# Gated delta rule in a fused decoder: gates as a process, weights split two units ahead, longer planned times for transfers, the turn bank's hold counted

## The chip, the cores and the metric
One core of a Trainium2 chip runs the whole program; the other cores are idle. The metric is the device time of one launch in microseconds, smaller is better. The core has a matrix engine (PE, with a weight-load stage PEld), VectorE (DVE), ScalarE (ACT), GpSimd (POOL), and SyncE (SP), whose queue issues most transfers. Engines run side by side, each takes its own instructions strictly in order, and they wait for each other by semaphores.

## The reference
Three decoder blocks, one after the other, on 512 tokens of width 1024, float32. The change lies in the second layer of the first block, `parallel_mixers`: a gated delta rule with 8 heads of 128 (tokens in chunks), beside a gated convolution of 31 taps over 1024 channels. Cut to that part:

```
proj = h @ w_in                      # qkv | z | a | bt | glu | gates
qkv = silu(causal_depthwise_conv(qkv, gdn_conv_qkv))          # 4 taps
g = -exp(gdn_a_log) * softplus(a + gdn_dt_bias); beta = sigmoid(bt)   # the decay gates: 16 columns of proj
gc = cumsum(g within a chunk); decay = exp(gc_i - gc_j) for i >= j
m = strict_lower((k*beta) k^T * decay)
u, w = solve(I + m, v*beta), solve(I + m, k*beta*exp(gc))
per chunk: v_new = u - w S;  o = (q*exp(gc)) S + (q k^T * decay) v_new
           S = S*exp(gc_last) + (k*exp(gc_last - gc))^T v_new
o = rms_norm(o) * silu(z)
c = c_lin * sigmoid(c_gate)          # the GLU: two halves of proj for each channel
c = silu(layer_norm(causal_depthwise_conv(c, conv_dw_w) + conv_dw_b))
y = sigmoid(g_a) * (o @ w_gdn_out) + sigmoid(g_c) * (c @ w_conv_out + b_conv_out)
```

## The kernel before
Every large product is made of three matmuls on split operands (`mm3`, lines L212 to L214: x by wl, x by wh twice): a weight tile of 1024 x 128 is loaded raw (`wr`, two buffers, SP's queue, `wload`, L353), cast to its high part `wh` on ACT (`split`, L346), and its low part `wl` is made by a subtraction (L347), in this stage on POOL, elsewhere on DVE. `wh` and `wl` have four buffers each.

The stage "gdn" is written as *units* and *processes*. A unit is one product of 1024 x 128 weights with all 512 tokens: 24 matmuls into one PSUM bank. There are 53 units after the start: q, k, v of heads 1 to 7 (`gdn_rows`), 16 GLU halves (`glu_conv`), 8 of z (`gdn_z`), 8 of output gates (`gdn_gate`). A process is a generator for the small, latency-bound work: it emits some instructions and yields a time in ns after which it may go on. `step` runs the process that is due, else three matmuls of the current unit. The clock of this planner is `pe_ns`, a sum of assumed PE times (680 ns for a triple, 230 for a small matmul, 110 for a turn); order of emission is order of execution on every engine except SP's queue (`keep_order`). So a yield is a number of PE nanoseconds, in the planner's count, that other work fills.

What the words stand for:
- *gates* (`gdn_gates`): the 16 columns a, bt become `small` (tile gsmall): beta, the cumulated decays (by matmuls with `triu` and `ones`) and their exponentials; they also go to DRAM as `gcrow`, from where each head's decay rows are fetched.
- *post* in `gdn_rows`: the 4-tap convolution (L824, L826), silu (L830, L833), a *turn* (four transposes, `four_turned`, L218) into the single PSUM bank of tag tp, from which ACT then copies (L837, L847) or sums squares (L814).
- *pairs*: for two heads at a time `gdn_decay`, then `gdn_blocks` (16 x 16 blocks inverted on DVE after a trip through DRAM: sm, sy, sx), `gdn_join` (blocks joined to 128 x 128), `gdn_head` (the recurrence and the final z product, L1052).
- *taps*: the 31-tap convolution is 30 DVE instructions per channel block (L654) and 8 blocks; `fill_dve` emits them one at a time wherever the planner thinks DVE is behind PE. Those left when all units are done are emitted behind the loop.
- *mix2*: the stage behind it starts with the products of the last gates (`gate_proj`, its low parts on DVE), then transposes the convolution's rows (`conv_norm`, L693), which need every tap done.

`split_ahead(2)` makes `wload` for the next units when one begins; a unit whose `may` is false is passed over for others, and one that comes up without its weights gets them on the spot:

```
        for u in ([u for u in units if u["may"]()] + units)[:n]:
            if u["w"] is None and sum(e["w"] is not None for e in units) < 3:
                u["w"] = wload(*u["src"])
```

Of the kernel before, what the change touches and what calls it, by code (L numbers as in the profile page):

```python
# [25 lines left out]
JOIN_NS, CHUNK_NS = 1300.0, 1300.0  # L26
# [82 lines left out]
def kernel(ctx: ExitStack, tc: tile.TileContext, a: dict, out: bass.AP, upto=99):  # L109
    nc = tc.nc  # L110
    V, A, G, PE, S = nc.vector, nc.scalar, nc.gpsimd, nc.tensor, nc.sync
    pe_ns, dve_ns = [0.0], [0.0]
# [181 lines left out]
    def unit(src, body, may=lambda: True):  # L294
        units.append({"src": src, "body": body, "may": may, "w": None})
# [341 lines left out]
    def glu_conv(c):  # L637
# [43 lines left out]
        unit((w, 0, 8, 4112 + 1024 + c * 128, 128), body, lambda: bool(ps))  # L681
# [40 lines left out]
    def gdn_gates():  # L722
# [3 lines left out]
        h, l = wload(w, 0, 8, 4096, 16)  # L726
        p = bank()
        for k in range(8):
            mm3(p[:16], (h[:, k], l[:, k]), (act.hi(k), act.lo(k)), k == 0, k == 7)
        ab = work("xr", (128, T))  # L730
        A.copy(ab[:16], p[:16])
        pt = tbank()
        for tt in range(4):
            PE.transpose(pt[:, tt, :16], ab[:16, tt * 128:(tt + 1) * 128], ident[:16, :16])
# [9 lines left out]
        V.tensor_tensor(u, u, z, OP.min)  # L744
        A.activation(u, u, AF.Exp)
        V.tensor_scalar(s2, u, 2.0, None, OP.add)
# [10 lines left out]
        ea = tiny((128, 8))  # L757
        A.activation(ea, alog, AF.Exp)
        V.scalar_tensor_tensor(sm(4), sm(4), -1.0, ea[:, None, :].to_broadcast([128, 4, 8]), OP.mult, OP.mult)
        pc = tbank((128, T))  # L760
        mm(pc[:, 0:32], triu, acc)
        mm(pc[:, 32:64], ones, acc)
        V.tensor_copy(small[:, 5], pc[:, 0:32])
        pr = tbank((128, T))
        PE.transpose(pr[:32, :128], small[:, 5], ident)
        row = t1()
        V.tensor_copy(row[:32], pr[:32, :128])
        gd["rows"] = dpool.tile([32, 128], FT, name="gcrow")
        S.dma_start(gd["rows"], row[:32])
# [7 lines left out]
        yield  # L777
# [9 lines left out]
    def gdn_rows(h):  # L787
# [18 lines left out]
        def four_turned(x):  # L806
            p = tbank()
            for c in range(4):
                turn(p[:, c], x[:, c], ident)
            return p  # L810
# [5 lines left out]
        def post(i, p):  # L816
# [18 lines left out]
            q = four_turned(xf)  # L835
# [9 lines left out]
            else:  # L845
# [7 lines left out]
                yield 3500.0  # L853
                A.copy(kq[:, :, 0], four_turned(s_))
# [27 lines left out]
    def gdn_decay(h):  # L882
        dt_ = t2((128, 4, 128))
        src = gd["rows"][0:1, 0:1]
        A.dma_start(dt_, bass.AP(tensor=src.tensor, offset=src.offset + h * 128, ap=[[0, 128], [1024, 4], [1, 128]]))
        yield 4000.0
# [22 lines left out]
    def gdn_blocks(h):  # L909
# [10 lines left out]
        yield 4000.0  # L920
# [20 lines left out]
        yield 4000.0  # L941
# [1032 lines left out]
    with ExitStack() as outer:  # L1974
        outer.enter_context(room(dict(ma=12)))
        mark("gdn")
        with room(vk=6, mt=4, at=4, Y=4, X=2, pad=2, xr=3, sq=1, t2=4, sqc=1, gsmall=1, ub=1, yb=1, tb=1):
            sq, lev = work("xr", (128, 3, 128)), work("sqc", (128, 2, 128))
# [12 lines left out]
            run(gdn_start(), gdn_gates())  # L1991
            banks(pj=3, tp=1, gt=3, cv=1)
            gdn_rows(0)
# [151 lines left out]
```

## Time and profile before

| | us |
|---|---|
| three runs: lowest, median, highest | 2883.54, 2889.5, 2892.16 |
| the profiled execution, its own time | 2888.98 |
| its span, first to last instruction | 2887.2 |
| PE busy over the span | 2704.2 (94%) |
| stage gdn and the first products of mix2, up to the last tap | about 402 to 1008 of the span |
| mean granted clock of TensorE | 0.966 |

The span is cut into stages by `mark`, and only the stretch from 402 to 1008 us differs between the two programs. The rows below have times in us from the span's start. In a timeline the bracket says how long the engine was idle just before the row and what ended that. [...]

### The profile page before, as it was taken

What the parts mean: (1) busy time and instruction counts of PE and PEld (TensorE: products, weight loads), DVE (VectorE), ACT (ScalarE), POOL (GpSimd) and SP (SyncE); (2) the same over time, 40 slices, a digit from 0 to 9 for tenths busy, and PEclk for the clock granted to TensorE, in tenths of its full rate; (3) what the DMA queues carried; (4) which work ended last, traced back from release to release, by engine and by line L of the source; (5) the groups of instructions that cost most, each with busy time, mean ns of one, the idle gap of its engine ahead of it and who ended that gap; (6) DMA issues with size and microseconds to landing.
All of it is one profiled execution on the core that took longest, in us unless ns stands there. A gap on an engine that the chain in (4) does not pass through costs nothing. (4 is left out here: it accounts for less than half of the span.)

```text
span 2887.2 us, 34809 instructions
## 1 busy us (share of the span) xinstructions
PE 2704.2 (94%) x13600; PEld 2193.2 (76%) x13600; DVE 1368.0 (47%) x2460; ACT 1066.4 (37%) x1999; POOL 477.7 (17%) x357
## 2 busy tenths in 40 slices
PE   9999978888889599999999999999999999999998
PEld 8888856667677488888888877776687777788887
DVE  3232354555546855655323256476454564622324
ACT  4222225444434242352322235455145564332231
POOL 0101025333333001101110121022001100311010
PEclk9999989889899799999999999999999999999999
DMA  5223334436454433444323323322235222443322
GB/s 187 95 99 98 95 90 78 76 63 72 62 89 43 75 99 126 125 147 146 110 95 96 102 94 113 111 59 82 71 100 99 56 70 74 130 141 97 101 95 80
DMA packets 330420, 277.30 MB, mean 96 GB/s; under 512 B 50360, under 2 KB 282512, under 8 KB 330256
## 3 DMA queue, kind: packets, MB, share of 16 engines
q1 hardware_dynamic: 292816, 251.22, 33.5%
q10 hardware_dynamic: 37440, 23.86, 2.7%
q8 instruction: 107, 1.75, 0.2%
q14 instruction: 57, 0.47, 0.1%
HBM read 256.64 MB, written 20.49 MB: 96 GB/s over the span
## 5 line engine op out<-in xcount | busy, mean ns | idle before, releaser
L212 PE MATMUL mm<-x,wl 128*128 128x512 f32 (+3 forms) x2072 | 813.5, 393 | 41.2 <-POOL wl L347 37.1
L347 DVE TENSOR_TENSOR wl<-wr,wh 128x1024 fp32r<-128x1024 f32 (+1 forms) x351 | 428.4, 1221 | 794.3 <-ACT wh L346 793.1
L213 PE MATMUL mm<-x,wh 128*128 128x512 f32 (+3 forms) x2072 | 798.7, 385 | 0.0
L214 PE MATMUL mm<-x,wh 128*128 128x512 f32 (+3 forms) x2072 | 797.7, 385 | 0.0
L346 ACT CAST wh<-wr 128x1024 fp32r<-128x1024 f32 (+2 forms) x425 | 436.3, 1027 | 804.4 <-PE mm L214 488.6
L212 PEld LDWEIGHTS mm<-x,wl 128*128 128x128 f32 (+2 forms) x2072 | 398.8, 192 | 120.4 <-POOL wl L347 40.6
L214 PEld LDWEIGHTS mm<-x,wh 128*128 128x128 f32 (+2 forms) x2072 | 398.5, 192 | 77.2 <-issue 1.9
L213 PEld LDWEIGHTS mm<-x,wh 128*128 128x128 f32 (+2 forms) x2072 | 399.8, 193 | 70.3 <-issue 1.4
L347 POOL TENSOR_TENSOR wl<-wr,wh 128x1024 fp32r<-128x1024 f32 x74 | 176.7, 2392 | 577.1 <-ACT wh L346 562.8
L347 POOL TENSOR_TENSOR h<-t,h 128x512 fp32r<-128x512 f32 x66 | 101.7, 1541 | 838.6 <-ACT h L346 838.6
L214 PE MATMUL mm<-wh,h 128*128 128x512 f32 x528 | 205.6, 389 | 0.0
L212 PE MATMUL mm<-wh,h 128*128 128x512 f32 x528 | 205.5, 389 | 0.0
L213 PE MATMUL mm<-wl,h 128*128 128x512 f32 x528 | 205.5, 389 | 0.0
L654 DVE SCALAR_TENSOR_TENSOR mm<-pad,cols,mm 128x512 f32<-128x512 f32 x232 | 174.7, 753 | 22.6 <-ACT mm L650 17.0
L214 PEld LDWEIGHTS mm<-wh,h 128*128 128x128 f32 x528 | 99.1, 188 | 20.6
L212 PEld LDWEIGHTS mm<-wh,h 128*128 128x128 f32 x528 | 99.1, 188 | 20.5
L213 PEld LDWEIGHTS mm<-wl,h 128*128 128x128 f32 x528 | 99.1, 188 | 20.5
L566 ACT ACTIVATE t<-mm 128x512 f32<-128x512 f32 x66 | 39.5, 599 | 127.9 <-PE mm L214 127.9
L826 DVE SCALAR_TENSOR_TENSOR xr<-mm,cols,xr 128x511 f32<-128x511 f32 (+2 forms) x72 | 53.8, 748 | 65.6 <-ACT xr L824 64.0
L567 DVE SCALAR_TENSOR_TENSOR t<-t,mm 128x512 f32<-128x512 f32 x66 | 45.4, 688 | 78.2 <-POOL h L347 54.9
L212 PE MATMUL mm<-m,wl 128*128 128x512 f32 (+1 forms) x224 | 81.6, 364 | 0.2 <-DVE g L1116 0.2
L214 PE MATMUL mm<-m,wh 128*128 128x512 f32 (+1 forms) x224 | 81.3, 363 | 0.0
(455 smaller groups left out, 3736.5 us busy)
## 6 DMA issues: line engine op xcount, KB each, us to landing
wr<-in_w_in SPq DMA_DIRECT2D x122, 512.0 KB
wr<-in_ffn_wg SPq DMA_DIRECT2D x44, 512.0 KB
wr<-in_ffn_wu SPq DMA_DIRECT2D x44, 512.0 KB
wr<-in_ffn_wd SPq DMA_DIRECT2D x44, 512.0 KB
wr<-in_w_ffn_in SPq DMA_DIRECT2D x44, 512.0 KB
wr<-in_w_ffn_out SPq DMA_DIRECT2D x22, 512.0 KB
xd<-m ACTq DMA_DIRECT2D x32, 256.0 KB
wr<-in_w_xkv SPq DMA_DIRECT2D x16, 512.0 KB
```

Of the source, the lines that this page charges most:

```text
L212: PE.matmul(o, lh[1], rh[0], start=start, stop=False)
L213: PE.matmul(o, lh[0], rh[1], start=False, stop=False)
L214: PE.matmul(o, lh[0], rh[0], start=False, stop=stop)
L346: A.copy(hi, src)
L347: (eng or V).tensor_sub(lo, src, hi.bitcast(FT))
L566: A.activation(sg, ps[0][f], AF.Silu)
L567: V.scalar_tensor_tensor(sg, sg, scale, ps[1][f], OP.mult, OP.mult)
L654: V.scalar_tensor_tensor(p if j < 30 else o, pad[:, j:j + T], tap31(j, c), p, OP.mult, OP.add)
L826: V.scalar_tensor_tensor(x[:, d:], p[:, :T - d], tap(3 - d), x[:, d:], OP.mult, OP.add)
```

## The change
The gates' product becomes a unit and their arithmetic a process (`gdn_decays`), which yields between its steps, so that units are emitted between them; its row of decays is issued from ACT's queue instead of SP's. Everything that reads the gates waits by a flag in the planner. The second half of a GLU pair may start (and have its weights split) at any time, and `split_ahead(2)` is called once before the loop. Yields get longer: joins and chunks 1300 to 1700, the decay rows 4000 to 6000, the blocks 4000 to 5000, Y and X 4000 to 7000, the turn of k 3500 to 5000. `tp_free` keeps the planner's time at which the turn bank will be read out; a turn waits for it. Two constants move from a buffer of xr to one of t2.

```diff
-JOIN_NS, CHUNK_NS = 1300.0, 1300.0
+JOIN_NS, CHUNK_NS = 1700.0, 1700.0
...
         unit((w, 0, 8, 4112 + c * 128, 128), body)
-        unit((w, 0, 8, 4112 + 1024 + c * 128, 128), body, lambda: bool(ps))
+        unit((w, 0, 8, 4112 + 1024 + c * 128, 128), body)
...
         dtb, alog = bcast_row("gdn_dt_bias", 8), bcast_row("gdn_a_log", 8)
-        h, l = wload(w, 0, 8, 4096, 16)
-        p = bank()
-        for k in range(8):
-            mm3(p[:16], (h[:, k], l[:, k]), (act.hi(k), act.lo(k)), k == 0, k == 7)
-        ab = work("xr", (128, T))
+
+        def body(h, l):
+            p = bank()
+            for k in range(8):
+                mm3(p[:16], (h[:, k], l[:, k]), (act.hi(k), act.lo(k)), k == 0, k == 7)
+                yield 1
+            spawn(post(p))
+
+        unit((w, 0, 8, 4096, 16), body)
...
+    def gdn_decays(p, dtb, alog):
+        ab = t2()
         A.copy(ab[:16], p[:16])
+        ea = tiny((128, 8))
+        A.activation(ea, alog, AF.Exp)
+        yield 1500.0
         pt = tbank()
+        tp_free[0] = pe_ns[0] + 4000.0
         for tt in range(4):
-            PE.transpose(pt[:, tt, :16], ab[:16, tt * 128:(tt + 1) * 128], ident[:16, :16])
+            turn(pt[:, tt, :16], ab[:16, tt * 128:(tt + 1) * 128], ident[:16, :16])
...
+        yield 1500.0
         A.activation(u, u, AF.Exp)
+        yield 2500.0
...
+        yield 6000.0
         pc = tbank((128, T))
+        tp_free[0] = pe_ns[0] + 3000.0
         mm(pc[:, 0:32], triu, acc)
         mm(pc[:, 32:64], ones, acc)
         V.tensor_copy(small[:, 5], pc[:, 0:32])
-        pr = tbank((128, T))
-        PE.transpose(pr[:32, :128], small[:, 5], ident)
-        row = t1()
-        V.tensor_copy(row[:32], pr[:32, :128])
-        gd["rows"] = dpool.tile([32, 128], FT, name="gcrow")
-        S.dma_start(gd["rows"], row[:32])
...
-        yield
+        yield 3000.0
+        pr = tbank((128, T))
+        turn(pr[:32, :128], small[:, 5], ident)
+        row = t1()
+        A.copy(row[:32], pr[:32, :128])
+        yield 1000.0
+        gd["rows"] = dpool.tile([32, 128], FT, name="gcrow")
+        A.dma_start(gd["rows"], row[:32])
+        yield 3000.0
+        gd["gates"] = True
...
-        def four_turned(x):
+        def four_turned(x, held):
             p = tbank()
+            tp_free[0] = pe_ns[0] + 440.0 + held
...
-            q = four_turned(xf)
+            yield from until(lambda: tp_free[0] <= pe_ns[0] and "beta" in gd)
+            q = four_turned(xf, 2500.0 if i == 0 else 1500.0)
...
-                yield 3500.0
-                A.copy(kq[:, :, 0], four_turned(s_))
+                yield 5000.0
+                yield from until(lambda: tp_free[0] <= pe_ns[0] and "kd" in gd)
+                A.copy(kq[:, :, 0], four_turned(s_, 1500.0))
...
     def gdn_decay(h):
+        yield from until(lambda: "gates" in gd)
...
-        yield 4000.0
+        yield 6000.0
...
         G.memset(yb.rearrange("p a b -> p (a b)")[:, ::17], 1.0)
-        yield 4000.0
+        yield 5000.0
...
                 gd["decay", h + i].append(m)
-        yield 4000.0
+        yield 7000.0
...
-            sq, lev = work("xr", (128, 3, 128)), work("sqc", (128, 2, 128))
+            sq, lev = t2((128, 3, 128)), work("sqc", (128, 2, 128))
...
-            run(gdn_start(), gdn_gates())
+            run(gdn_start())
             banks(pj=3, tp=1, gt=3, cv=1)
             gdn_rows(0)
+            gdn_gates()
             spawn(gdn_pair(0))
...
+            split_ahead(2)
             while True:
```

Where instructions stand, at three places. First PE at the stage's start, before: the last matmul of the gates' own product (mm_2795), their turn, the sums with triu and ones (L208), the turn to rows (L765), and then the first unit, the GLU half mm_2911.

```order
L214 MATMUL mm_2795<-x_2456,wh_2790 16x512
L734 MATMUL mm_2822<-ident,xr_2820 128x16 x4
L208 MATMUL mm_2858<-gsmall_2827,xr_2606 128x32 x2
L765 MATMUL mm_2862<-ident,gsmall_2827 32x128
L212 MATMUL mm_2911<-x_2444,wl_2895 128x512
L213 MATMUL mm_2911<-x_2445,wh_2894 128x512
```

Now the turn (of t_2852) stands inside the first GLU half, here mm_2862, and the sums stand 48 matmuls of units later, inside the unit mm_2962:

```order
L214 MATMUL mm_2862<-x_2444,wh_2796 128x512
L218 MATMUL mm_2872<-ident,t_2852 128x16 x4
L212 MATMUL mm_2862<-x_2444,wl_2797 128x512
L213 MATMUL mm_2862<-x_2445,wh_2796 128x512
L214 MATMUL mm_2862<-x_2444,wh_2796 128x512
```

```order
L214 MATMUL mm_2962<-x_2444,wh_2857 128x512
L208 MATMUL mm_2973<-gsmall_2877,t_2606 128x32 x2
L212 MATMUL mm_2962<-x_2444,wl_2858 128x512
L213 MATMUL mm_2962<-x_2445,wh_2857 128x512
L214 MATMUL mm_2962<-x_2444,wh_2857 128x512
```

So no two steps of the gates stand next to each other on PE any more; 12 matmuls lie between the sums and the next turn.

Second POOL at the same place, before: the low parts of the weights in the order in which they are made. wl_2895 is that of the first GLU half, wl_2945 that of its second half; L887 adds the mask to the decay rows of heads 0 and 1, which come from DRAM.

```order
L347 TENSOR_TENSOR wl_2895<-wr_2893,wh_2894 128x1024
L347 TENSOR_TENSOR wl_2901<-wr_2899,wh_2900 128x1024
L347 TENSOR_TENSOR wl_2907<-wr_2905,wh_2906 128x1024
L887 TENSOR_TENSOR t_2891<-t_2891,sqc_2607 128x512
L887 TENSOR_TENSOR t_2918<-t_2918,sqc_2607 128x512
L347 TENSOR_TENSOR wl_2945<-wr_2943,wh_2944 128x1024
```

Now the two halves' are wl_2797 and wl_2820:

```order
L347 TENSOR_TENSOR wl_2797<-wr_2795,wh_2796 128x1024
L347 TENSOR_TENSOR wl_2820<-wr_2818,wh_2819 128x1024
L347 TENSOR_TENSOR wl_2858<-wr_2856,wh_2857 128x1024
L347 TENSOR_TENSOR wl_2900<-wr_2898,wh_2899 128x1024
L347 TENSOR_TENSOR wl_2958<-wr_2956,wh_2957 128x1024
L667 TENSOR_TENSOR ma_2952<-ma_2952,xr_2954 128x512
```

The second half's low part moved from behind two weights and two mask additions to right behind the first's. The same holds for the other GLU pairs; one weight in the stage (the z product of head 4) is still made where its unit starts.

Third DVE at the stage's end, before: the last two heads' z products (L1052) and the taps and low parts (L347, of the first products of mix2) behind them.

```order
L1052 SCALAR_TENSOR_TENSOR ma_6545<-mm_6618,cols_286,ma_6545 128x512
L654 SCALAR_TENSOR_TENSOR mm_6416<-pad_6413,cols_300,mm_6416 128x512
L1052 SCALAR_TENSOR_TENSOR ma_6545<-mm_6631,cols_286,ma_6545 128x512
L654 SCALAR_TENSOR_TENSOR mm_6416<-pad_6413,cols_300,mm_6416 128x512 x13
L347 TENSOR_TENSOR wl_6864<-wr_6862,wh_6863 128x1024
L654 SCALAR_TENSOR_TENSOR mm_6416<-pad_6413,cols_300,mm_6416 128x512
```

Now (L1075 is the z product there):

```order
L1075 SCALAR_TENSOR_TENSOR ma_6564<-mm_6652,cols_286,ma_6564 128x512
L1075 SCALAR_TENSOR_TENSOR ma_6564<-mm_6658,cols_286,ma_6564 128x512
L654 SCALAR_TENSOR_TENSOR ma_4940<-pad_6337,cols_300,mm_6340 128x512
L654 SCALAR_TENSOR_TENSOR mm_6687<-pad_6684,cols_293,mm_6687 128x512 x10
L347 TENSOR_TENSOR wl_6864<-wr_6862,wh_6863 128x1024
L654 SCALAR_TENSOR_TENSOR mm_6687<-pad_6684,cols_293,mm_6687 128x512 x4
```

Behind the second z product 75 taps stood, and 61 stand now; eight low parts lie among them in both. On PE only six matmuls of a unit are left between the last head's last product (L208, with at) and its final turn, where 30 stood.

## Rows read from the trace of the kernel before

**Rows 1.** The page: busy time of the engines over the span, share, instructions.
```profile
PE 2704.2 (94%) x13600; PEld 2193.2 (76%) x13600; DVE 1368.0 (47%) x2460; ACT 1066.4 (37%) x1999; POOL 477.7 (17%) x357
```

**Rows 2.** Stretches of the stage: start:end, length, busy time (and instructions) of each engine, granted clock, share of the DMA engines, GB/s.
```profile
402.00:426.00 24.00, 7.42 (x33) 3.65 (x32) 11.80 (x40) 7.73 (x13) 2.70 (x2) 0.69 0.05 12
426.00:922.00 496.00, 419.42 (x2233) 341.20 (x2233) 260.29 (x531) 224.29 (x545) 185.58 (x127) 0.88 0.49 71
...
950.50:978.00 27.50, 27.45 (x121) 22.64 (x122) 24.94 (x32) 6.89 (x8) 0.00 (x0) 1.00 0.76 106
978.00:1008.50 30.50, 1.32 (x9) 0.79 (x8) 27.40 (x37) 6.39 (x12) 0.00 (x0) 0.55 0.09 26
```

**Rows 3.** What PE waited for from 427 to 922: us in total, times, longest.
```profile
PE mm L212 <- POOL wl L347: 29.1, 8, 5.7
PE mm L208 <- DMA X<-sx: 10.1, 2, 5.1
PE mm L218 <- ACT t L814: 9.0, 6, 2.4
PE mm L218 <- ACT Y L992: 6.2, 2, 3.6
PE mm L208 <- ACT t L1017: 5.2, 2, 4.2
...
PE mm L218 <- POOL sq L852: 4.4, 2, 4.0
```

**Rows 4.** PE in order of time around the gates.
```profile
406.89 0.39 PE L214 MATMUL mm<-x,wh 128*16 128x512 f32 x1
407.94 0.41 PE L734 MATMUL mm<-ident,xr 16*128 16x16 f32 x4 [0.67 <-ACT xr L731]
418.18 1.03 PE L208 MATMUL mm<-gsmall,xr 128*128 128x32 f32 x4 [9.82 <-issue]
...
425.70 0.79 PE L212 MATMUL mm<-x,wl 128*128 128x512 f32 x1 [5.81 <-POOL wl L347]
```

**Rows 5.** PE inside one unit, at the clock's lower level (start to start) and, four microseconds later, at the higher.
```profile
428.00 0.63 PE L214 MATMUL mm<-x,wh 128*128 128x512 f32 x1
428.43 0.63 PE L212 MATMUL mm<-x,wl 128*128 128x512 f32 x1
...
432.64 0.39 PE L212 MATMUL mm<-x,wl 128*128 128x512 f32 x1
432.87 0.39 PE L213 MATMUL mm<-x,wh 128*128 128x512 f32 x1
```

**Rows 6.** Three stretches in which the granted clock was at its lower level throughout (columns as in rows 2).
```profile
411.00:431.50 20.50, 7.23 (x19) 5.57 (x20) 9.34 (x35) 4.50 (x9) 4.66 (x2) 0.50 0.29 53
...
622.80:643.00 20.20, 15.89 (x64) 11.55 (x65) 6.68 (x9) 5.99 (x14) 2.35 (x1) 0.50 0.17 26
759.50:772.80 13.30, 12.86 (x57) 9.37 (x58) 8.95 (x12) 8.70 (x18) 2.37 (x1) 0.50 0.07 10
```

**Rows 7.** One weight from its issue on SP's queue to its cast and its low part; then the unit of the second GLU half, and the z product of head 4, which wait for theirs.
```profile
425.67 0.37 SPq L353 DMA_DIRECT2D wr<-in_w_in  x1
431.09 1.05 ACT L346 CAST wh<-wr 128x1024 fp32r<-128x1024 f32 x1 [6.91 <-DMA wr<-in_w_in]
432.21 2.40 POOL L347 TENSOR_TENSOR wl<-wr,wh 128x1024 fp32r<-128x1024 f32 x1 [4.24 <-ACT wh L346]
439.76 0.79 PE L212 MATMUL mm<-x,wl 128*128 128x512 f32 x1 [5.60 <-POOL wl L347]
831.69 0.80 PE L212 MATMUL mm<-x,wl 128*128 128x512 f32 x1 [5.74 <-POOL wl L347]
```

**Rows 8.** A cast that waits for its transfer, the PE instruction behind it, and the stretch around them (columns as in rows 2).
```profile
684.78 1.04 ACT L346 CAST wh<-wr 128x1024 fp32r<-128x1024 f32 x1 [7.83 <-DMA wr<-in_w_in]
686.15 0.58 PE L208 MATMUL mm<-t,vk 128*128 128x128 f32 x1 [4.15 <-ACT t L1017]
660.00:700.00 40.00, 30.29 (x139) 25.24 (x138) 18.79 (x36) 11.92 (x28) 16.21 (x11) 0.89 0.91 84
```

**Rows 9.** The fetch of X for heads 0 and 1 (issue) and its first reader; a step of a join on 32 x 32 blocks.
```profile
523.04 2.36 ACTq L939 DMA_DIRECT2D X<-sx  x2
531.14 1.22 PE L208 MATMUL mm<-X,mt 128*128 128x128 f32 x4 [4.98 <-DMA X<-sx]
876.00 1.48 PE L208 MATMUL mm<-Y,X 32*32 32x32 f32 x32 [2.82 <-ACT X L982]
```

**Rows 10.** PE at the end of head 6: the last product and the final turn.
```profile
913.00 0.38 PE L208 MATMUL mm<-t,at 128*128 128x128 f32 x2
920.07 0.60 PE L218 MATMUL mm<-ident,t 128*128 128x128 f32 x4
```

**Rows 11.** DVE behind the last z product, and the last channel block.
```profile
922.60 0.75 DVE L1052 SCALAR_TENSOR_TENSOR ma<-mm,cols,ma 128x512 f32<-128x512 f32 x1 [0.49 <-PE mm L218]
...
944.22 1.23 DVE L347 TENSOR_TENSOR wl<-wr,wh 128x1024 fp32r<-128x1024 f32 x1 [10.70 <-ACT wh L346]
...
984.66 22.92 DVE L654 SCALAR_TENSOR_TENSOR mm<-pad,cols,mm 128x512 f32<-128x512 f32 x29 [0.91 <-ACT mm L650]
```

**Rows 12.** PE there: the transposes that need all taps.
```profile
983.81 0.47 PE L693 MATMUL mm<-ident,ma 128*128 128x128 f32 x1 [5.04 <-DVE ma L654]
1008.42 0.47 PE L693 MATMUL mm<-ident,ma 128*128 128x128 f32 x1 [24.14 <-DVE ma L654]
```

More of the change, by code (lines that the diff above doesn't have):

```diff
@@ L111 @@
     V, A, G, PE, S = nc.vector, nc.scalar, nc.gpsimd, nc.tensor, nc.sync
-    pe_ns, dve_ns = [0.0], [0.0]
+    pe_ns, dve_ns, tp_free = [0.0], [0.0], [0.0]
     n_names = [0]
@@ L725, in gdn_gates, with post @@
         dtb, alog = bcast_row("gdn_dt_bias", 8), bcast_row("gdn_a_log", 8)
-        h, l = wload(w, 0, 8, 4096, 16)
-        p = bank()
-        for k in range(8):
-            mm3(p[:16], (h[:, k], l[:, k]), (act.hi(k), act.lo(k)), k == 0, k == 7)
-        ab = work("xr", (128, T))
+        def body(h, l):
[5 more added lines that the diff above has]
+        unit((w, 0, 8, 4096, 16), body)
+        def post(p):
+            yield from gdn_decays(p, dtb, alog)
+    def gdn_decays(p, dtb, alog):
+        ab = t2()
         A.copy(ab[:16], p[:16])
+        ea = tiny((128, 8))
+        A.activation(ea, alog, AF.Exp)
+        yield 1500.0
         pt = tbank()
+        tp_free[0] = pe_ns[0] + 4000.0
         for tt in range(4):
-            PE.transpose(pt[:, tt, :16], ab[:16, tt * 128:(tt + 1) * 128], ident[:16, :16])
+            turn(pt[:, tt, :16], ab[:16, tt * 128:(tt + 1) * 128], ident[:16, :16])
         small = work("gsmall", (128, 8, 32))
@@ L756, in gdn_gates @@
         V.scalar_tensor_tensor(acc, acc, 2.0, z, OP.mult, OP.add)
-        ea = tiny((128, 8))
-        A.activation(ea, alog, AF.Exp)
         V.scalar_tensor_tensor(sm(4), sm(4), -1.0, ea[:, None, :].to_broadcast([128, 4, 8]), OP.mult, OP.mult)
+        yield 6000.0
         pc = tbank((128, T))
+        tp_free[0] = pe_ns[0] + 3000.0
         mm(pc[:, 0:32], triu, acc)
```

## The prediction, made before the changed kernel ran
> **What bounds the kernel now.** I read the page first, then a table of stretches, then who waits for whom, then the order in time at the places named. PE is busy for 94% of the span [rows 1], so a gain has to come out of PE's idle time or out of matmuls that ran on a slow clock. Only 402 to 1008 us differs between the programs, and there both are to be had. From 402 to 426 PE is busy 7.4 of 24 us, from 426 to 922 419.4 of 496, and from 978 to 1008.5 1.3 of 30.5 [rows 2]. So 16.6 us and 76.6 us are idle, 93.2 in sum, before the last head's z product on DVE at 922.60 [rows 11]. Behind it comes a tail in which DVE, not PE, sets the end: from 950 to 1008 DVE is busy 52.3 of 58 us [rows 2], and PE waits 24.14 us for the last tap [rows 12].
>
> The clock is the second cost. [...] Three such stretches are busy 36.0 of 54.0 us, 67% [rows 6]. In two of them PE was idle for 13.3 and 4.3 us (length less busy time), in the third for 0.4 only. That the clock falls with the waits is therefore my assumption, borne out by two of three; where it holds, a wait costs more than its length. DVE (260 of 496 us), ACT (224) and POOL (186) have room [rows 2].
>
> **The change part by part.**
>
> *Gates.* Between the gates' product and the first unit PE waits 0.67, 9.82 and 5.81 us [rows 4]. The 9.82 is the chain on DVE and ACT between turn and sums. Now 48 matmuls of units stand between the two: 48 x 0.23 = 11.0 us (the higher level of [rows 5]), against 10.2 from turn to sums [rows 4]. That covers it by a hair. The 5.81 is the first unit's low part, whose cast stood on ACT behind the whole chain; it is now made ahead of it. I take 14.6 of 16.6 as gone. Bounds: all of it; or only the 5.81, if the DVE operations of the posts between them stretch the chain by as much as it has cover.
>
> *Weights split two units ahead.* Eight waits of PE for a low part on POOL sum to 29.1 us [rows 3]. From issue to cast a weight takes 5.4 us, then cast and subtraction 1.05 and 2.40 [rows 7]; split at its own unit, the last two stand bare before PE, with whatever is queued on POOL. A second GLU half waits 5.60 us [rows 7]. Seven of the eight units are now split ahead, one (head 4's z, 5.74 us [rows 7]) is not: 23.4 gone. Bounds: 0, if the wait only changes its name (first rival), and 29.1.
>
> With two raw buffers a weight can come every (5.4 + 1.05 + 2.40)/2 = 4.4 us, and a unit lasts 24 x 0.23 = 5.5. So the supply suffices while transfers run undisturbed. [...]
>
> *The turn bank's hold.* PE waits 9.0 us in six turns for the sums of squares that still read the bank, and 4.4 for k's scaling on POOL [rows 3]. The planner now keeps the bank for 1500 to 2500 ns and gives k's turn 1500 ns more; the time goes to unit matmuls. I take 7 and 3 as gone. Bounds: 0 and 13.4.
>
> *Longer times.* X is waited for twice, 10.1 us in all [rows 3], 4.98 of it once, with 8.1 us from issue to first reader [rows 9]. 3 us more of planned work take 3 from each: 6.0. Joins (6.2 for the turn of Y alone) and chunks gain little: in the order of the change the steps of two heads still stand with a few unit matmuls between them, and the planner counts 230 ns for each 32 x 32 matmul, of which 32 take 1.48 us in fact [rows 9]. I take 2.0. Bounds: 0 and 11.4 (6.2 + 5.2 [rows 3]).
>
> *What is new.* Six matmuls are left between head 6's last product and its final turn, 1.4 us; that chain lasts 7.1 us [rows 10], filled until now. So about 5.7 us of idle time arise, and head 7's turn, behind it, adds 0.8: 6.5. Every chain that was just covered while PE ran slowly is less covered when PE runs faster; no row shows these waits. Between 0 and 24.8 us (the four waits of [rows 3] that are neither weights nor X: 9.0 + 6.2 + 5.2 + 4.4) I take 8, nearer to nothing, because most yields grew.
>
> *Moved without cost.* The decay row's issue goes from SP to ACT, under 0.4 us there; SP's weights no longer queue behind it. The two constants in t2 cost nothing as long as four buffers suffice; they hide behind the start.
>
> **The sum.** Idle time gone: 14.6 + 23.4 + 7 + 3 + 6 + 2 = 56.0; new: 14.5; net 41.5 of 93.2, and 51.7 are left. If the time at the low clock shrinks with the idle time, it goes from 134 to 74 us; 60 x 0.67 x 0.47 = 19 us. Head 7's z product now stands ahead of the whole unit in which it stood halfway: 12 matmuls, 2.8 us. Up to the z product that is 63 us.
>
> The tail: 61 taps are left behind the z product instead of 75; at 22.92/29 = 0.79 us each [rows 11] that is 11 us. The 10.70 us for which DVE waits on the first low part of mix2 [rows 11] should shrink, because the last gates' weights are loaded while PE waits for heads 6 and 7; I take half, 5. Bounds: 0 and 8.7. Below, PE cannot be the end: four units and 120 matmuls, 216 x 0.23, are 50 us, and the tail stays near 70. So 16 us, and 79 in all. The profiled execution took 2888.98 us, against a median of 2889.5, so the sum holds for either: **2810 us**. A us of idle time is worth (41.5 + 19)/41.5 = 1.46 us here.
>
> **Rivals.**
>
> *The wait for weights moves to ACT.* A cast that stands earlier may find its transfer not landed; ACT then stands, and whatever is behind it. At 684.78 a cast waits 7.83 us for its transfer, and PE 4.15 us for the ACT instruction behind it; the DMA engines are busy 0.91 there, for only 84 GB/s [rows 8]. Two such per pair of heads are 8 x 4.15 x 1.46 = 48 us: gain 31, 2858 us. [...]
>
> *The same, and slower.* From 13 such waits (79 / (4.15 x 1.46)) out of the stage's 50-odd casts the gain is gone. With 16 the time is 18 us above before: 2907. Against it: over the second stretch the DMA share is 0.49 [rows 2].
>
> *The allowances don't land.* The planner's ns are not PE's ns (the 32 x 32 matmuls). Then the bank's hold, k's scaling, X, joins and chunks stay: 18 x 1.46 = 26 us less, 2836.
>
> *Nearly all stalls go.* If 25 us of idle time are left instead of 51.7, 26.7 x 1.46 = 39 us and 4 of the tail come on top: 2767.
>
> *Nothing happens.* The stage's end is set by a DVE chain; were DVE the bound all along, PE's gain would come back as a longer wait for the taps. DVE's 260 of 496 us speak against it.
>
> **How the numbers follow.** Forecast (2785 to 2838): 0.58. Waits moved to ACT, still faster: 0.13. Slower by them: 0.05. Allowances don't land: 0.12. Nearly all go: 0.10. Nothing: 0.02. A difference under 0.3% (9 us, about the spread of the runs shown) can't be told from none. Faster 0.93, same 0.02, slower 0.05. The range of 2772 to 2850 takes in the forecast, the allowances, about half of the case above and half of the case below.
>
> **What would show it.** Right: from the gates' product to the first unit no gap above 2 us; one wait of PE of more than 4 us on a low part; the two waits for X at 2 us; a wait of about 6 us at the final turns; the stretch from 402 us to the last z product near 457 us, now 520.6 [rows 11]; the clock's share above 0.93 in it; the tail from z product to last tap near 70 us, now 86. Wrong: casts on ACT waiting for transfers more than three or four times; waits of PE for DVE; a low clock that stays although the waits are gone; or a tail that is no shorter.

## The result and the profile after

The changed kernel takes 2797.82 us (median of 4 runs, 2795.27 to 2799.53) against 2886.52 us before: a ratio of 0.969, 95% interval 0.967 to 0.971. That is faster, within the stated range and 12 us below the stated 2810. The profiled execution took 2799.25 us, its span is 2797.5, 89.7 us shorter than before.

First the page's busy times, which answer to [rows 1]:

```profile
PE 2673.2 (96%) x13600; PEld 2170.6 (78%) x13600; DVE 1375.7 (49%) x2459; ACT 1065.4 (38%) x2000; POOL 477.5 (17%) x357
```

Then the stretches of [rows 2]: from 402 us to the last z product, now at 855.91, and from there to the last tap (start:end, length, busy time and instructions of PE, PEld, DVE, ACT, POOL, granted clock, share of the DMA engines, GB/s). The granted clock is TensorE's, as a share of its full speed. Of the 520 stretches of 1 us from 402 to 922 in the kernel before, 371 have 1.00, 121 have 0.50, and 28 a mean between the two; of the 453 up to 855 in the changed kernel, 393, 47 and 13. These two levels are the upper and the lower clock below.

```profile
402.00:426.00 24.00, 21.28 (x98) 15.48 (x96) 10.90 (x33) 15.48 (x23) 10.92 (x6) 1.00 0.47 85
402.00:855.90 453.90, 399.79 (x2276) 324.95 (x2275) 284.33 (x577) 231.61 (x559) 190.72 (x129) 0.94 0.56 79
855.91:919.53 63.62, 51.38 (x222) 42.12 (x221) 56.37 (x71) 21.29 (x30) 3.71 (x4) 0.90 0.47 83
```

PE is busy 21.3 of the first 24 us, 7.4 before. Up to the z product the stretch went from 520.6 to 453.9 us, its idle time from 93.2 to 54.1. The clock's share is 0.94 where it was 0.69 and 0.88. The tail, DVE's part, went from 85.8 to 63.6 us. Work behind the last tap takes as long as before (1878.0 us to the span's end, 1878.8 before).

The units are shared out differently, too. Behind the last z product, up to the last tap, the middle matmul of a triple (x by wh, L213) stands 76 times before and 72 times now (count, busy time, mean ns). So four triples, half a unit, moved from the tail into the stretch ahead of it.

```profile
L213 PE MATMUL mm<-x,wh 128*128 128x512 f32 x76 | 29.6, 389 | 0.0
L213 PE MATMUL mm<-x,wh 128*128 128x512 f32 x72 | 28.7, 399 | 0.0
```

What PE waits for in that stretch, to be held against [rows 3] (us in total, times, longest):

```profile
PE mm L208 <- ACT t L1040: 9.2, 4, 6.4
PE mm L208 <- DMA X<-sx: 9.1, 4, 5.4
PE mm L218 <- POOL t L1068: 8.1, 3, 4.7
PE mm L212 <- POOL wl L347: 5.9, 1, 5.9
PE mm L208 <- ACT X L1005: 4.2, 4, 3.0
PE mm L218 <- ACT Y L1015: 4.0, 2, 3.0
PE mm L218 <- ACT t L834: 3.3, 2, 2.7
PE mm L218 <- ACT sq L868: 2.8, 1, 2.8
```

One wait for a low part is left of eight; X is waited for nearly as long as before, in four pieces instead of two; the row behind POOL's t L1068 is new, and the recurrence (t L1040, t L1017 before) went from 5.2 to 9.2. Of the new 8.1 us, 6.3 stand before heads' final turns and 1.75 before a turn of k (sq, at 676.06 below).

PE in order of time: the gates' product, the only wait left of the gates' chain (the turn to rows, behind squares that read the same bank), the longest wait of the recurrence, the turn of k, the weight that is still split at its own unit, a head's final turn, those of heads 6 and 7, and the wait for the last tap.

```profile
405.46 0.40 PE L214 MATMUL mm<-x,wh 128*16 128x512 f32 x1
426.07 0.39 PE L218 MATMUL mm<-ident,gsmall 128*32 128x128 f32 x1 [2.79 <-ACT sq L868]
...
641.95 0.79 PE L208 MATMUL mm<-t,vk 128*128 128x128 f32 x2 [6.37 <-ACT t L1040]
...
676.06 0.63 PE L218 MATMUL mm<-ident,sq 128*128 128x128 f32 x4 [1.75 <-POOL t L1068]
...
765.39 0.80 PE L212 MATMUL mm<-x,wl 128*128 128x512 f32 x1 [5.88 <-POOL wl L347]
...
789.33 0.66 PE L218 MATMUL mm<-ident,t 128*128 128x128 f32 x4 [1.61 <-POOL t L1068]
...
853.62 2.25 PE L218 MATMUL mm<-ident,t 128*128 128x128 f32 x8 [4.74 <-POOL t L1068]
...
919.58 0.69 PE L693 MATMUL mm<-ident,ma 128*128 128x128 f32 x2 [12.29 <-DVE ma L654]
```

Four of the stretches in which the granted clock was at 0.50 throughout; they lie at the waits of 6.37, 5.88, 4.74 and 12.29 us:

```profile
638.00:647.00 9.00, 5.05 (x17) 4.47 (x18) 1.76 (x5) 0.62 (x2) 0.00 (x0) 0.50 0.64 110
764.00:770.00 6.00, 4.61 (x13) 3.84 (x14) 0.00 (x0) 0.73 (x2) 4.88 (x3) 0.50 0.57 86
853.00:859.00 6.00, 5.36 (x16) 4.27 (x17) 4.16 (x6) 1.55 (x3) 4.12 (x5) 0.50 0.23 51
911.00:920.00 9.00, 0.42 (x3) 0.42 (x3) 8.64 (x12) 0.52 (x1) 0.00 (x0) 0.50 0.00 0
```

DVE behind the last z product, against [rows 11]: the first low part of mix2 no longer waits 10.70 us.

```profile
855.91 0.75 DVE L1075 SCALAR_TENSOR_TENSOR ma<-mm,cols,ma 128x512 f32<-128x512 f32 x1 [0.39 <-PE mm L218]
...
866.04 2.25 DVE L347 TENSOR_TENSOR wl<-wr,wh 128x1024 fp32r<-128x1024 f32 x1
...
873.11 1.23 DVE L347 TENSOR_TENSOR wl<-wr,wh 128x1024 fp32r<-128x1024 f32 x1 [1.78 <-ACT wh L346]
```

### The profile page after: what moved, and what is told of

Read it like the earlier page. It is cut to its first block, busy times and chain, and to the rows that moved or that the text cites. A ratio compares the mean times of both kernels' runs of the same rounds, so it can differ in the third digit from the quotient of the medians.

```text
span 2797.5 us, 34810 instructions
## 1 busy us (share of the span) xinstructions
PE 2673.2 (96%) x13600; PEld 2170.6 (78%) x13600; DVE 1375.7 (49%) x2459; ACT 1065.4 (38%) x2000; POOL 477.5 (17%) x357
## 3 DMA queue, kind: packets, MB, share of 16 engines
q8 instruction: 107, 1.75, 0.3%
## 5 line engine op out<-in xcount | busy, mean ns | idle before, releaser
L347 DVE TENSOR_TENSOR wl<-wr,wh 128x1024 fp32r<-128x1024 f32 (+1 forms) x351 | 429.4, 1224 | 784.5 <-ACT wh L346 783.3
L213 PE MATMUL mm<-x,wh 128*128 128x512 f32 (+3 forms) x2072 | 792.8, 383 | 0.0
L214 PEld LDWEIGHTS mm<-x,wh 128*128 128x128 f32 (+2 forms) x2072 | 394.5, 190 | 75.9 <-issue 1.8
L213 PEld LDWEIGHTS mm<-x,wh 128*128 128x128 f32 (+2 forms) x2072 | 395.6, 191 | 68.4 <-issue 1.4
L347 POOL TENSOR_TENSOR wl<-wr,wh 128x1024 fp32r<-128x1024 f32 x74 | 177.0, 2394 | 543.9 <-ACT wh L346 521.6
L347 POOL TENSOR_TENSOR h<-t,h 128x512 fp32r<-128x512 f32 x66 | 101.6, 1539 | 837.0 <-ACT h L346 837.0
L213 PE MATMUL mm<-wl,h 128*128 128x512 f32 x528 | 205.6, 389 | 0.0
L212 PEld LDWEIGHTS mm<-wh,h 128*128 128x128 f32 x528 | 99.1, 188 | 20.6
L213 PEld LDWEIGHTS mm<-wl,h 128*128 128x128 f32 x528 | 99.1, 188 | 20.4
L214 PE MATMUL mm<-m,wh 128*128 128x512 f32 (+1 forms) x224 | 81.3, 363 | 0.0
L213 PE MATMUL mm<-m,wh 128*128 128x512 f32 (+1 forms) x224 | 81.0, 362 | 0.0
```

The source lines that it names most:

```text
L212: PE.matmul(o, lh[1], rh[0], start=start, stop=False)
L213: PE.matmul(o, lh[0], rh[1], start=False, stop=False)
L214: PE.matmul(o, lh[0], rh[0], start=False, stop=stop)
L347: (eng or V).tensor_sub(lo, src, hi.bitcast(FT))
```

## The experiments

The change has three parts: weights (GLU halves, `split_ahead` before the loop), gates (the process), times (longer yields and the bank's hold). Six kernels (e1, e2, e4, e3, e8, e7) and the two given ones hold every combination of them. The table has the median, the ratio to the kernel before with its interval, and from each profile: PE's idle time from 402 us to the last z product (length less busy time), the time at the lower clock, 0.50, in it (twice one minus the granted clock, summed over stretches of 1 us), and the tail from the z product to the end of the last tap. Then PE's idle time by cause: up to 432 us (start); and from there to the z product, summed by what PE was waiting to do, low parts (wl), readers of the turn bank and what is turned there, k among it (bank), X and Y and the joins' steps (XY), the recurrence (rec), the heads' final turns (end).

| kernel | us | ratio | idle | clock 0.50 | tail | start | wl | bank | XY | rec | end |
|---|---|---|---|---|---|---|---|---|---|---|---|
| before | 2887 | 1 | 93.2 | 136 | 85.8 | 16.6 | 29.1 | 17.6 | 21.5 | 8.0 | 0 |
| e1: weights | 2855.8 | 0.989 (0.988 to 0.990) | 70.4 | 113 | 86.1 | 11.4 | 5.7 | 15.5 | 26.6 | 10.5 | 0 |
| e2: gates | 2884.2 | 0.999 (0.998 to 1.000) | 85.9 | 126 | 86.1 | 8.1 | 25.1 | 18.5 | 20.6 | 11.4 | 0 |
| e4: times | 2850.6 | 0.987 (0.985 to 0.988) | 84.3 | 110 | 64.1 | 16.6 | 30.6 | 8.1 | 14.2 | 8.0 | 6.3 |
| e3: weights, gates | 2856.4 | 0.989 (0.987 to 0.990) | 68.2 | 106 | 85.6 | 3.2 | 5.7 | 17.2 | 27.2 | 14.0 | 0 |
| e8: weights, times | 2818.6 | 0.975 (0.974 to 0.977) | 59.6 | 70 | 64.1 | 8.9 | 6.1 | 8.4 | 19.3 | 10.1 | 6.3 |
| e7: gates, times | 2832.3 | 0.981 (0.979 to 0.982) | 74.2 | 81 | 62.5 | 8.1 | 28.0 | 12.0 | 11.6 | 7.3 | 6.7 |
| changed kernel | 2797.8 | 0.969 (0.967 to 0.971) | 54.1 | 55 | 63.6 | 2.8 | 5.9 | 7.7 | 20.0 | 10.9 | 6.3 |
| e5: joins, chunks 1300 | 2823.4 | 0.977 (0.976 to 0.979) | 53.7 | 73 | 74.7 | 2.8 | 5.7 | 13.1 | 15.8 | 11.9 | 3.7 |
| e6: no hold | 2805.0 | 0.972 (0.970 to 0.974) | 56.4 | 62 | 61.4 | 3.2 | 6.0 | 13.2 | 17.2 | 10.1 | 6.4 |
| c1: low parts on POOL | 2779.4 | 0.962 (0.960 to 0.963) | 48.8 | 55 | 50.9 | 2.8 | 5.9 | 8.4 | 15.9 | 8.9 | 6.3 |

Two profiles of one order differ, too. Up to the z product every engine has the same instructions in the same order in the changed kernel and in c1, and PE's idle time is 54.1 and 48.8 us. And the work behind the last tap, which none of the first ten kernels' edits touches, took 1878.0 to 1882.3 us in them. So a difference of up to 5 us between two profiles says little.

**Weights alone (e1).**

```diff
-        unit((w, 0, 8, 4112 + 1024 + c * 128, 128), body, lambda: bool(ps))
+        unit((w, 0, 8, 4112 + 1024 + c * 128, 128), body)
...
+            split_ahead(2)
             while True:
```

> The kernel before, with nothing but the weights' edit: the second GLU half may start at any time, and split_ahead(2) is called before the loop. Theory (the parts add up, each by the idle time it takes from PE): the waits of PE for a low part, 29.1 us before and 5.9 us in the changed kernel, go to 4 to 8 us here, 23 us less; with the clock's share of 0.6 us for each us of idle time (the two profiles: 39 us of idle time and 23 us of clock) that is 37 us, so 2850 against 2886.5; and if the 10.7 us for which DVE waits on the first low part of mix2 come from the same cause, up to 10 more, 2840. Rival (waits change their name): PE's idle time falls by less than 10 us because PE then waits for casts that stand on ACT for their transfers, over 2870. Rival (the gain needs all parts): within 10 us of before.

2855.8: 31 us, a little less than the 37. The wait for low parts went as foretold, and with it 5 of the start: units now stand ahead of the gates' sums. But X took 5.5 us back (10.1 before), the first of these rows of PE's waits up to the z product, and the tail did not move.

```profile
PE mm L208 <- DMA X<-sx: 15.6, 3, 6.1
PE mm L218 <- ACT t L814: 8.9, 6, 2.4
...
PE mm L212 <- POOL wl L347: 5.7, 1, 5.7
```

**Gates alone (e2).** The changed kernel with weights and times undone; of the diff these lines, with all of `gdn_decays`, stay:

```diff
-            run(gdn_start(), gdn_gates())
+            run(gdn_start())
...
+            gdn_gates()
```

> The kernel before, with the gates as a process alone (unit, yields, flags, decay row on ACT's queue, constants in t2); weights, times and the bank's hold as before. Theory (the parts add up): the 16.3 us of waits between the gates' product and the first unit fall to 3 as in the changed kernel, 13.5 us x 1.6 = 21 us, 2865. As the second GLU half still may not start early, its wait of 5.6 us and the other low parts' stay. Rival: the chain only moves, since the posts behind it still wait for beta and the decay rows; 2880 or above. Rival (planner's order decides by chance): a time outside 2855 to 2880 with waits of PE in places that no part of the edit touches.

2884.2, nothing that can be told from before, and the first rival's number (2880 or above). The chain is covered, but the unit behind it, a second GLU half, waits longer for its weight than the two waits of [rows 4] and [rows 7] did each, and the recurrence waits 3.4 us more:

```profile
421.38 0.80 PE L212 MATMUL mm<-x,wl 128*128 128x512 f32 x1 [7.59 <-POOL wl L347]
```

**Times alone (e4).** All yields and `tp_free` of the diff in the kernel before, from the joins' to X's:

```diff
-JOIN_NS, CHUNK_NS = 1300.0, 1300.0
+JOIN_NS, CHUNK_NS = 1700.0, 1700.0
...
+            yield from until(lambda: tp_free[0] <= pe_ns[0])
...
-        yield 4000.0
+        yield 7000.0
```

> The kernel before, with the longer yields and the turn bank's hold alone. Theory (the parts add up): of PE's idle time little goes, about 2.4 us net in the changed kernel's profile when weights (23.2) and gates (13.5) are taken off its 39.1, 4 us with the clock; but the order has 63 taps left behind the last z product, 75 before: 12 x 0.79 = 9.5 us, and the half unit behind head 7, 2.8 us. So 2870, waits for low parts still near 29 us. Rival (the times give the weights their time: a longer yield lets the planner begin units earlier and so split earlier): waits for low parts under 18 us, and under 2855. Rival: nothing, 2880 or more.

2850.6, 20 us better than expected, by two things: the tail is 21.7 us shorter, so the 10.7 us wait on the first low part hangs on the times; and the bank and the joins with X and Y took 16.8 us less of PE's time, of which the new waits at the heads' final turns gave 6.3 back. The low parts stayed, so the rival's mechanism is out although its number (under 2855) came true. PE's waits:

```profile
PE mm L212 <- POOL wl L347: 36.4, 9, 6.1
...
PE mm L218 <- POOL t L1048: 8.1, 3, 4.7
...
PE mm L208 <- DMA X<-sx: 2.2, 1, 2.2
```

**The changed kernel without the weights (e7), without the times (e3), without the gates (e8).** Each takes one of the three pieces above back out; e7:

```diff
-        unit((w, 0, 8, 4112 + 1024 + c * 128, 128), body)
+        unit((w, 0, 8, 4112 + 1024 + c * 128, 128), body, lambda: bool(ps))
...
-            split_ahead(2)
```

> The changed kernel with the weights' edit undone: the second GLU half waits for the first, no split_ahead before the loop. The order of the taps is that of the changed kernel (61 behind the last z product). Theory: waits for low parts come back, 23 us more idle time of PE and 37 us in all, 2835; if the wait of DVE for the first low part of mix2 hangs on it, up to 2845. Rival (the low parts are in time for another reason, more planned work between units): under 2815.

2832.3, as the theory has it; tail 62.5, so it does not hang on the weights. X is hardly waited for:

```profile
PE mm L208 <- DMA X<-sx: 0.6, 1, 0.6
```

> The changed kernel with the longer times and the bank's hold undone, so weights and gates together. Theory (the tail hangs on the times alone: from the last z product to the last tap 64.1 and 62.5 us in the two kernels with the new times, 85.8 to 86.1 in the three without): tail 86 us here. And since the weights alone already took the 9.8 us wait for the gates' chain off PE (its place is taken by units that start earlier), the gates add little to them: 2845 to 2855. Rival (the gates need the weights' edit, without which the unit behind them waits 7.6 us for its low part): 2838 or less. Rival (the tail hangs on the weights and gates together): tail under 75 us.

2856.4, 1 us above the theory's range, with a tail of 85.6: with the weights the gates are worth nothing in the median, and the tail is the times' alone.

> The kernel before with weights and times and the bank's hold, gates as before. Theory (the parts overlap at the stage's start but add otherwise): the gates are worth 18 us with the times (2850.6 to 2832.3) and little with the weights, so 2798 to 2816; the stretch from 402 us to the last z product 454 to 470 us, tail 62 to 64. Rival (weights and times simply add): 2819. Rival (the gates alone carry the part by which the three together are worth more than their sum, 89 against 71): 2826 or more.

2818.6, just outside the theory and on the rival's number: weights and times add up (31 + 37 = 68), and the gates, worth 3 alone and nothing with the weights, give 18 (e4 to e7) and 21 (e8 to the changed kernel) once the times are there. The 21 are 18 by the ratios, and 15 by the spans, as e8's profiled run took 2814.0. Without the times XY, bank and recurrence took back what the gates freed (e3 against e1: start 8.2 less, the three together 5.8 more); with them they did not (changed kernel against e8: start 6.1 less, the three 0.8 more). These sums are differences of single profiles and near what two profiles of one order differ by. That the gates need the times is shown by the medians; the mechanism is not.

**Joins and chunks (e5).**

```diff
-JOIN_NS, CHUNK_NS = 1700.0, 1700.0
+JOIN_NS, CHUNK_NS = 1300.0, 1300.0
```

> The changed kernel with joins and chunks back at 1300 ns. Theory: in the stage 2 us of idle time with the clock 3 us, and in the tail 10 taps more behind the last z product (71 against 61 in the order) x 0.79 = 8 us: 2809. Rival (the waits for X, Y and the recurrence, 20 us in the changed kernel, would be far longer without): PE's waits behind X, Y and L1040 over 30 us, 2815 or more. Rival (no worth): within 4 us of 2798.

2823.4: 26 us slower by the medians, 22 by the spans, over the theory's 11; the number is the rival's, but its waits (behind X, Y and the recurrence) did not grow (27.7 us against 30.9). The tail is 11.1 us longer (10 taps and a wait of 4.5). In the stretch the idle time did not change, but more of it came in waits for the bank, with more time at the lower clock (73 us against 55), and PE's busy time rose by 9 us (410.2 against 399.8, less 1.4 of the gates' product). Of all the stretches of 1 us, PE was busy 59.7 us at the lower clock, against 40.3; times 0.47 (one less 0.23/0.43, the starts in [rows 5]) that is 9 us too, so the clock accounts for it:

```profile
PE mm L218 <- ACT ma L876: 8.7, 3, 6.8
PE mm L208 <- ACT t L1040: 8.6, 3, 6.4
```

**The bank's hold (e6).**

```diff
-            yield from until(lambda: tp_free[0] <= pe_ns[0] and "beta" in gd)
+            yield from until(lambda: "beta" in gd)
...
-                yield from until(lambda: tp_free[0] <= pe_ns[0] and "kd" in gd)
+                yield from until(lambda: "kd" in gd)
```

> The changed kernel without the turn bank's hold: turns no longer wait for tp_free, all yields as in the changed kernel. 60 taps stand behind the last z product in its order, 61 in the changed kernel, so the tail stays at 63 us. Theory (the hold is what keeps a turn from waiting for the bank): PE's waits for the bank's readers, 5.9 us from 432 us on in the changed kernel and 17.6 before, come back to 13 to 17; 7 to 11 us with the clock's share are 11 to 18: 2809 to 2816. Rival (the longer yields alone keep the turns apart): under 9 us of such waits, and within 5 us of 2798.

2805.0, 7 us slower by the medians, its interval just meeting that of the changed kernel, and under the theory's 2809. Of 5.1 us by the spans 3.3 lie behind the last tap, where nothing was edited, so that the hold is worth time is not shown. The bank's waits went from 17.6 to 13.2 by the yields, and from there to 7.7 by the hold, as the theory has it at its lower end; the expectation's 5.9 left out the turn of k, 1.75. But X, the joins and the recurrence took 3.6 us less than in the changed kernel, so that idle time rose by 2.3 only. The two longest waits at the bank without the hold:

```profile
505.28 1.11 PE L218 MATMUL mm<-ident,ma 128*128 128x128 f32 x4 [4.82 <-ACT ma L850]
...
683.63 0.63 PE L218 MATMUL mm<-ident,sq 128*128 128x128 f32 x4 [3.81 <-POOL t L1068]
```

**Low parts of the next stage on POOL (c1).** The tail tested by taking DVE's other work out of it:

```diff
             for left in background[1]:
                 left()
-            now["lo"] = V
...
             run(gate_proj("gcx", "w_in", 7184, acts["b1_1"], None, "mf"))
+            now["lo"] = V
```

> The changed kernel with the low parts of the eight weights of the first products of mix2 on POOL instead of DVE. Theory (DVE alone sets the end of the tail): 8 x 1.22 = 9.8 us of DVE's work and 5.5 us of its waits for casts go, so the last tap comes up to 15 us sooner; PE, which waits 12.3 us for it, then has its own work as the limit: 12 us, and about 2 of the clock behind the wait, 2784. Rival (DVE and POOL slow each other: a low part on DVE took 2.25 us beside one on POOL against 1.22 alone): the taps beside POOL take longer, 2790 to 2795. Rival (PE now waits for POOL's low parts, 2.40 us each): 2797 or more.

2779.4, faster than both kernels. In the tail PE is now busy without a gap (first row, the stretch from z product to last tap), and 29 taps on DVE, beside POOL's low parts, take the 22.9 us that they took in [rows 11]:

```profile
851.02:901.88 50.86, 50.86 (x220) 41.88 (x220) 46.75 (x62) 16.47 (x21) 21.92 (x12) 0.97 0.58 93
```

```profile
853.36 22.93 DVE L654 SCALAR_TENSOR_TENSOR mm<-pad,cols,mm 128x512 f32<-128x512 f32 x29 [0.93 <-ACT mm L650]
```

So DVE was the tail's limit, and 12.8 us went with it. The other 5 are idle time in the stretch, where the order is the same and X was waited for less (9.1 in the changed kernel); why is open.

```profile
PE mm L208 <- DMA X<-sx: 4.9, 3, 3.2
```

**Three tries at what is left.** On top of c1: the unit with a loaded weight first (c4), both yields around the block trips longer (c2), the second of them alone (c5).

```diff
-            u = next((u for u in units if u["may"]()), None)
+            u = next((u for u in units if u["may"]() and u["w"] is not None), None) or next((u for u in units if u["may"]()), None)
```

```diff
-        yield 3500.0
+        yield 6500.0
         A.dma_start(ub, blocks(gd["sm"]))
...
                 gd["decay", h + i].append(m)
-        yield 7000.0
+        yield 9000.0
```

> As c1_pool_tail, but a unit whose weights are loaded goes ahead of one that has none, which concerns the z product of head 4 alone, the one weight still split at its own unit. Theory: its wait, 5.9 us, goes, with the low clock behind it (6.8 us) 9 us: 2770. Rival (the wait passes to the steps of head 4, which need that product): within 4 us of 2779.

2784.5 (2778.4 to 2791.5), no gain, and 1.5 us beyond the rival's range. In the profile, of a run of 2791.5, PE's wait of 5.9 us became one of 5.2 us at another unit, for a bank that ACT had not copied out, because ACT had stood for 8.74 us; for the last 6.4 of them it was issuing four transfers. ACT and then PE there:

```profile
780.63 0.94 ACTq L962 DMA_DIRECT2D Y<-sy  x2
781.61 5.39 ACTq L962 DMA_DIRECT2D X<-sx  x2
787.05 0.60 ACT L1088 ACTIVATE ma<-mm 128x512 f32<-128x512 f32 x1 [8.74 <-issue]
...
788.48 0.59 ACT L663 COPY ma<-mm 128x512 f32<-128x512 f32 x1
```

```profile
789.12 0.79 PE L212 MATMUL mm<-x,wl 128*128 128x512 f32 x1 [5.20 <-ACT ma L663]
```

> The changed kernel with the low parts of the next stage's first weights on POOL (as in c1_pool_tail, 2779.4 us), and two yields longer: 9000 for 7000 behind the fetch of Y and X, 6500 for 3500 ahead of the fetch of the blocks. Theory (these waits are a matter of the planner's time): PE's waits for X, 1.1 and 3.2 us and shorter ones, go, and so does the 5.9 us behind the ACT queue, whose issue of ub stood until mt had landed; 9 us x 1.5 = 13, 2766. The order has 51 taps left instead of 61, worth nothing here as PE is busy throughout that tail. Rival (each wait taken hands its time to the next, as X's did: 7 us gone with the times alone and back with the weights): idle time before the last z product within 4 us of 48.8, within 5 us of 2779. Rival (the heads' chain of steps grows and the end of heads 6 and 7 with it): over 2784.

2792.1: slower than c1, with 58.0 us idle, over 2784 as the second rival has it. X (1.8 us) and the longest wait of the recurrence (from 5.9 to 2.0) fell as meant; the bank's readers rose from 8.4 to 13.0 and the joins' steps from 11.0 to 18.7, while the heads' end, which the rival names, grew by 0.7 only.

> As c1_pool_tail (2779.4 us) with one yield longer: 9000 for 7000 behind the fetch of Y and X; of c2_x_ub's two yields the other stays at 3500. Theory (c2_x_ub lost its 13 us by the yield ahead of ub, which delays every pair's chain): X's waits fall from some 5 us to under 2, the others stay, idle time 45 us before the last z product and 2772 to 2777. Rival (any longer yield only moves which steps meet each other, so waits for the bank and for the steps of a join come in place of X's): idle time 49 us or more, 2782 to 2792, with X's waits under 2 us all the same.

2789.1: the rival. X is down to 1.2 us, idle time is 53.5 (458.85 less 405.36):

```profile
402.00:860.85 458.85, 405.36 (x2278) 327.59 (x2277) 278.91 (x579) 232.71 (x561) 189.87 (x130) 0.93 0.57 78
```

```profile
694.95 1.11 PE L218 MATMUL mm<-ident,xr 128*128 128x128 f32 x4 [3.62 <-ACT xr L853]
```

## Why the prediction was right, point by point

The stretch to the z product was foretold to lose 63 us and lost 66.7, of which 1.4 lie ahead of the edit (the gates' product ended at 405.46 instead of 406.89; in c1, of the same order, at 406.88): 65.3. The tail lost 22.2 (16 foretold), and the whole span 89.7 (79 foretold). So the forecast was near, and what it says goes (idle time of PE, slow matmuls, the tail) is what went. But the parts of the first sum are further off than the sum.

*Idle time:* 39.1 gone, 41.5 foretold.

*The half unit:* this step has its sign wrong. The prediction takes 2.8 us off the stretch, because head 7's z product would stand ahead of the unit in which it stood halfway. It stands behind that unit: 76 triples were left behind it before and 72 are now. So the stretch has 12 matmuls, 2.8 us, more. The prediction's own count of the tail now (four units) is right.

*The clock:* PE's busy time in the stretch fell by 27.6 us, 26.2 without the 1.4. As 2.8 us of work were added, the clock gave back 29.0; 19 was foretold. Summed over stretches of 1 us, PE was busy 101.0 us at the lower clock before and 40.3 now, and 60.7 x 0.47 is 28.5, the same size. The forecast's 19 come from 134 us at the lower clock before, by the shares of [rows 2] 2 x 0.31 x 24 + 2 x 0.12 x 496 (136 over stretches of 1 us), and from 0.47, by the starts of [rows 5].

So 39.1 - 2.8 + 29.0 = 65.3 stands against 41.5 + 2.8 + 19 = 63.3. That the sums agree within 2 us is luck: the clock gave 10 us more, the half unit 5.6 and the idle time 2.4 less than foretold.

*Gates:* 13.8 us of idle time gone in the changed kernel, 14.6 foretold. By the runs 5 to 8 of these come by the weights' edit too (start 11.4 in e1, 8.9 in e8). *Weights:* 23.2 against 23.4, and the one wait left is head 4's z, as read from the order. *Bank's hold and k's scaling:* 9.9 against 10, of which by e6 4.4 come by the longer yields and 5.5 by the hold.

*X:* 6.0 foretold, 1.0 came in this profile, 5.2 in that of c1. The step that failed is taking 3 us from each of X's two waits as if the other edits left them alone. Without the weights' edit 3 us more of planned work do take the wait away (10.1 to 2.2 in e4, to 0.6 in e7). With it 4.9 to 9.1 stay (c1, e8, the changed kernel), and without the times it makes the wait longer (15.6 in e1, 16.2 in e3). That X's transfer had gone on while PE stood for a low part, so that one wait had covered another, fits this; no run shows it by itself. The prediction had such an effect as an unknown of 8 us for chains less covered, and put none of it on X. The recurrence rose by 2.9.

*Joins and chunks:* 2.0 of idle time foretold for the stretch. By e5 the edit is worth 9 us in the stretch and 11 in the tail, the first all by the clock and none by idle time. So the term was mis-sized; the tail's part was in the sum by its count of taps. *New at the heads' end:* 6.3 against 6.5, but 4.74 at heads 6 and 7, for which the 6.5 were worked out, and 1.61 at an earlier head.

*That the clock falls with the waits:* this held as far as their places tell. In the changed kernel ten waits of PE are 2.7 us or longer up to the last tap, and nine stretches at 0.50 lie at nine of them. The third stretch of [rows 6], which the prediction took for one without a wait, starts at 759.50; most of a wait of 2.61 us lies just ahead of it:

```profile
759.94 0.63 PE L218 MATMUL mm<-ident,Y 64*64 64x64 f32 x4 [2.61 <-ACT Y L992]
```

But the time at the lower clock is not in proportion to the idle time (136 for 93.2, 55 for 54.1, 113 for 70.4 in e1, 81 for 74.2 in e7), so the ratio that the prediction used for it failed: it made 134 to 74 of what was 136 to 55. A us of idle time was worth (39.1 + 29.0)/39.1 = 1.74, not 1.46. The 0.6 of clock for each us, with which the expectations of e1 and e2 work, has the half unit's wrong sign in it; it is 0.74 here.

*The tail:* 14 taps fewer, 11 us as foretold; of the 10.70 us wait half was expected to go, and nearly all did: the tail's waits on DVE went from 17.1 in sum to 5.5. They go with the times alone (e4). That fits the reason given, that weights come in while PE waits for heads 6 and 7, which was not tested apart. The half unit that moved out of the tail is another; alone it is not enough, for it has moved in e5 as well, where these waits are 9.5.

*The rival that the waits move to ACT* did not happen in the changed kernel, though its sign (more than three or four casts that wait for transfers) was there: up to the z product casts waited 6 times and 12.4 us (4 times and 19.0 before), and up to the last tap 9 times and 26.4 (12 times and 50.4 before). The longest wait of PE behind ACT has another cause (below).

## What to carry to other kernels

Sum the waits by cause, but do not add up the gains of edits as if each left the other waits alone (X: 5 to 9 us with all parts, 0.6 without the weights' edit). Check each term of the sum by what was measured for it: here two large errors nearly cancelled. Test an edit of several parts by its combinations; here one part was worth 3 us alone and some 20 with the others. Where a stage ends on another engine's queue, look at what that engine does there for someone else: moving eight low parts to an idle engine gave 13 us in the tail, and no retiming that was tried on top of it gave anything.

## What the runs showed of the hardware

Issuing transfers took ACT's time. In the changed kernel ACT is idle for 5.74 us at the four of Y and X, and the rows of their issue take 5.05 of these:

```profile
678.23 1.96 ACTq L962 DMA_DIRECT2D Y<-sy  x2
680.23 3.09 ACTq L962 DMA_DIRECT2D X<-sx  x2
683.37 0.69 ACT L844 ACTIVATE xr<-mm,cols 128x512 f32<-128x512 f32 x1 [5.74 <-issue]
```

And ACT stood at an issue that depends on an earlier transfer: here ub's fetch stands on ACT's queue while mt, issued at 627.17, is still being stored. ACT is idle for 7.40 us, and PE waits 6.37 us for the step of the recurrence behind it.

```profile
627.17 0.92 ACTq L929 DMA_DIRECT2D sm<-mt  x2
...
640.85 0.63 ACTq L940 DMA_DIRECT2D ub<-sm  x1
641.53 0.62 ACT L1040 ACTIVATE t<-mm,gsmall 128x128 f32<-128x128 f32 x2 [7.40 <-DMA sm<-mt]
```

In c4 the four issues of Y and X, 6.4 of ACT's 8.74 us, were in PE's way (5.20 us). These issues on a queue with less behind it would be the next thing to try; it was not tried.

A low part on DVE took 2.25 us beside one on POOL (866.04 above; POOL's took 2.40 from 864.81) and 1.23 and 1.22 where POOL was idle (873.11 above, and 877.28). The taps were not slowed by POOL in c1: the 29 from 853.36 took 22.93 us with four low parts on POOL beside them, 9.54 us in all, and 22.92 in [rows 11], where POOL was idle [rows 2]. Why the one is slowed and the other not is not shown.
